# A two-layer hybrid decoder trunk on one core: weight places 448 columns wide, compressed products on four column groups, the last tile's scores cut in two, and a new order table

## The chip, the cores and the metric

The kernel runs on one core of a Trainium2 chip. A core has five engines that run side by side, each through its own instructions in order: TensorE (PE, matrix products and transposes), VectorE (DVE), ScalarE (ACT), GpSimd (POOL) and SyncE (SP, here the one that starts nearly all loads and stores). They wait for one another by semaphores. TensorE multiplies a stationary operand, which it loads first (PEld, at most 128 columns), with a moving operand of at most 512 columns, and writes to PSUM, a small memory of 8 banks of 512 float32 columns; all other data lie in SBUF.

The metric is device time in microseconds (us) of one execution, as the median of several.

## The reference

512 tokens of width 1024 pass two layers. A layer normalizes x, multiplies by one wide matrix w_in, and hands the columns to four groups of mixers:

```python
h = rmsnorm(x, norm_w)
p = split_cols(h @ w_in)
o_a = dsa_mixer(...)       # ReLU indexer, top 128 keys of each query, softmax attention
o_b = nsa_mixer(...)       # compressed, selected and window attention, gated
o_c = shortconv_mixer(...) # b * conv3(c * x)
o_d = pool_mixer(...)      # pooling over 2, 4, 8, 16 tokens, minus the token, a product, a scale
x + concat(silu(gate) * o) @ w_out
```

Group B's compressed branch makes 32 (31 used) compressed keys and values out of blocks of 32 tokens at a stride of 16, each by one product with a 2048 x 64 matrix, and attends to them:

```python
blocks = tok[:, cmp_idx] + pe_cmp
return blocks.reshape(B, n_cmp, CMP_LEN * HEAD_DIM) @ w     # compress
s_c = jnp.einsum('bqhd,bnd->bhqn', qb, k_cmp) * scale
```

All values are float32, and the output must keep nearly that precision.

## The kernel before, in words

**Tiling.** Tokens are cut into 4 tiles of 128; the 1024 channels into 8 chunks of 128 (`KC`). To keep precision on fast products, an operand is split into a high part (rounded for the fast product) and a low part (the difference), and a product becomes three: high x high, high x low, low x high. ACT writes the high part, POOL or VectorE the low part (`lo`). `lin_tok` (lines 639 to 648) gives token-major results, `lin_ch` (650 to 658) channel-major ones, 24 products of up to 512 columns each. Weights come through `load_w` (580 to 606): two chunks at a time land in a place `st` (3 of them), and go from there to `wh` and `wl` (6 of each). All these places are 436 columns wide, the widest that a load needs, and hold two rows of 436 float32: the second begins 1,744 bytes in.

**The order.** The kernel's functions don't issue anything. They record instructions on a `Tape`, numbered from 0 in the order in which Python meets them (5,023 of them). `ORDER` (lines 180 to 437) lists all numbers in the order in which `play` (515 to 536) then issues them, and so fixes each engine's order, and which buffer of its kind each tile gets (`place`). Engines take their own instructions in that order; a wait at the head of an engine's queue holds everything behind it.

**A layer.** `projections` (1336) runs the indexer's, group A's and group B's projections, transposes the queries and keys, and computes the index scores. Then, in program order, come `compress` and `compressed`, the gates of A and B, `channel_constants` (in layer 0), attention of A and B tile by tile, with the top-k searches (`topk`, 16 rounds of VectorE's MAX8 and MATCH_REPLACE8) between them, convolution, pooling, and the output projection. The order table interleaves all that, so that TensorE has long products while softmax pieces come back from the other engines.

**Compressed products.** `compress` (1018) makes the two token streams `u` (keys s=0, values s=1). `compressed` (1035 to 1066) loads the 2 x 2048 x 64 matrices into four places (`wt` for the first 8 steps, `st` for the last 8) and does 16 steps t, with two full-precision products each: 32 stationary columns of `u`, 64 moving columns of weights, one for the keys into PSUM partitions 0 to 31 and one for the values into 32 to 63. `tape.after` chains them so that the two alternate. Then ACT copies keys (`zc`) and values (`vc`), POOL rotates the keys (`rope`), TensorE transposes them, and ACT and VectorE write them as high and low part into `kcT`, which is columns 0 to 31 of the key tile `kTB`, ahead of the 512 token keys.

**Scores.** `probs` (1079 to 1116) does one branch of one tile: per head two products (high and low key part) into a PSUM bank `s` of 512 columns, then one VectorE reduction that adds the mask, writes `pb` and leaves the extreme in `mn`, and the exponential on ACT. For tiles 1 and 2 of group B the 32 compressed keys and the up to 384 token keys of the selected branch fit one bank, and both come from one product (`cmp`). For tile 3 they would be 32 + 512 = 544 columns; so `att_b` (1195) gives it a second bank `sc` of kind `tr`, with two products of 32 columns for each head, and one VectorE sum of 128 columns (`e`) for all heads.

**The start.** 40 transposes of the identity (`warm`, 685) are recorded at the start and stand where the order table puts them; `spread` (692) transposes norm weights (`g_row`, loaded by ACT's queue) and spreads them over partitions.

Of the kernel before, what the change touches and what calls it, by code (L numbers as in the profile page):

```python
# [13 lines left out]
OP = mybir.AluOpType  # L14
# [157 lines left out]
class Engine:  # L172
# [367 lines left out]
def trunk(ctx: ExitStack, tc: tile.TileContext, x, norm_w, w_in, w_out, conv_w, pe_cmp, w_cmp_k, w_cmp_v,  # L540
# [39 lines left out]
    def load_w(src, segs, early=None, start=False):  # L580


        n = sum(c for _, c in segs)
        stage = res.tile([P, KC, 436], F32, name=nm("ws"), tag=early) if early else None

        def part(h):
            if early:
# [278 lines left out]
    def layer(l, hT, w_first, norm):  # L866
# [168 lines left out]
        def compressed(us):  # L1035
# [13 lines left out]
            for t in range(16):  # L1049
                for s in range(2):  # L1050
                    op = PE.matmul(pc[32 * s : 32 * s + 32, 0:HD], us[s][:, t::16], wts[2 * (t // 8) + s][:, t % 8, :],
                                   start=t == 0, stop=t == 15)
                    if before:
                        tape.after(op, before)
# [434 lines left out]
```

## Time and profile before

| what | value |
|---|---|
| median of 3 runs | 520.76 us (519.15 to 520.86) |
| the profiled execution | 520.58 us, of it span 518.8 us |
| mean granted TensorE clock | 0.998 |
| loads and stores | 50.06 MB, mean 96 GB/s |
| compressed products' records | 128 (64 a layer) |
| records of 32-column scores | 16 (8 a layer) |

The span runs from the first instruction to the last; the rest of the execution's time lies around it. A row of the timeline gives start, duration, engine, operation, `out<-in` by the names of the program, rows*columns of the stationary operand, the moving operand and a count. A row of the groups gives busy time and mean duration in ns, and behind the bar the idle time ahead of the group with what ended it. TensorE's products overlap one another, so the distance between starts, not the duration, tells what one costs.

### The profile page before, as it was taken

What the parts mean: (1) busy time and instruction counts of PE and PEld (TensorE: products, weight loads), DVE (VectorE), ACT (ScalarE), POOL (GpSimd) and SP (SyncE); (2) the same over time, 40 slices, a digit from 0 to 9 for tenths busy, and PEclk for the clock granted to TensorE, in tenths of its full rate; (3) what the DMA queues carried; (4) which work ended last, traced back from release to release, by engine and by line L of the source; (5) the groups of instructions that cost most, each with busy time, mean ns of one, the idle gap of its engine ahead of it and who ended that gap; (6) DMA issues with size and microseconds to landing.
All of it is one profiled execution on the core that took longest, in us unless ns stands there. A gap on an engine that the chain in (4) does not pass through costs nothing. (4 is left out here: it accounts for less than half of the span.)

```text
span 518.8 us, 8976 instructions
## 1 busy us (share of the span) xinstructions
PE 509.1 (98%) x2691; PEld 425.4 (82%) x2691; DVE 374.2 (72%) x1038; ACT 337.7 (65%) x840; POOL 316.4 (61%) x541
## 2 busy tenths in 40 slices
PE   8999999999999999999999999999999999999995
PEld 7998787888888888887888988877888888888885
DVE  5536999998888684872571599999984786868523
ACT  5889866444568877675478993464566787787522
POOL 5799843664375938747388972256456578584531
PEclk9999999999999999999999999999999999999999
DMA  7954531553321102205865431055241302022304
GB/s 245 246 116 128 124 97 22 140 138 79 79 58 36 61 23 63 61 27 153 283 188 150 111 92 31 2 151 127 52 119 32 92 1 65 18 81 62 134 9 162
DMA packets 73247, 50.06 MB, mean 96 GB/s; under 512 B 24680, under 2 KB 63728, under 8 KB 73200
## 3 DMA queue, kind: packets, MB, share of 16 engines
q1 hardware_dynamic: 72608, 48.45, 34.8%
q10 hardware_dynamic: 592, 1.05, 0.5%
q8 instruction: 21, 0.34, 0.3%
q14 instruction: 26, 0.21, 0.1%
HBM read 45.29 MB, written 4.19 MB: 95 GB/s over the span
## 5 line engine op out<-in xcount | busy, mean ns | idle before, releaser
L535 PE MATMUL mm<-hT,wh 128*128 128x512 f32 x544 | 172.8, 401 | 0.3 <-DVE sg L535 0.3
L535 POOL TENSOR_TENSOR wl<-st,wh 128x384 fp32r<-128x384 f32 (+2 forms) x116 | 110.0, 969 | 61.2 <-ACT wh L535 56.8
L535 PEld LDWEIGHTS mm<-hT,wh 128*128 128x128 f32 x544 | 100.4, 188 | 20.9 <-DVE sg L535 1.1
L535 PE MATMUL mm<-w,mT 128*128 128x512 f32 (+1 forms) x408 | 100.5, 385 | 0.3 <-DVE cd L535 0.3
L535 PE MATMUL mm<-hT,wl 128*128 128x512 f32 x272 | 98.9, 400 | 0.3 <-DVE sg L535 0.3
L535 PEld LDWEIGHTS mm<-w,mT 128*128 128x128 f32 x408 | 72.2, 188 | 15.0 <-DVE cd L535 0.5
L535 POOL TENSOR_TENSOR w<-st,w 128x512 fp32r<-128x512 f32 x48 | 61.8, 1300 | 21.8 <-ACT w L535 19.8
L535 ACT ACTIVATE wh<-st 128x768 fp32r<-128x768 f32 (+2 forms) x60 | 47.3, 790 | 24.1 <-DMA st<-in_w_in_dram 14.5
L535 PEld LDWEIGHTS mm<-hT,wl 128*128 128x128 f32 x272 | 50.6, 188 | 10.6 <-issue 0.4
L535 ACT ACTIVATE pb<-pb,mn 128x512 f32<-128x512 f32 (+3 forms) x96 | 53.2, 556 | 8.7 <-DVE mn L535 8.3
L535 PE MATMUL mm<-wh,hT 128*128 128x436 f32 (+1 forms) x224 | 52.9, 336 | 0.8 <-DVE vA L535 0.4
L535 POOL TENSOR_SCALAR pb<-pb,rs,gt 128x512 f32<-128x512 f32 (+3 forms) x64 | 38.4, 616 | 23.3 <-DVE rs L535 14.8
L535 DVE MAX8 m<-acc 128x8 f32<-128x384 f32 (+2 forms) x96 | 51.5, 551 | 0.8
L535 DVE MATCH_REPLACE8 acc<-m,acc 128x384 f32<-128x384 f32 (+2 forms) x96 | 51.9, 543 | 0.3
L535 PE MATMUL mm<-w,hT 128*128 128x512 f32 x192 | 51.9, 399 | 0.0
L535 DVE TENSOR_TENSOR pl<-tr,ph 128x512 fp32r<-128x512 f32 x60 | 40.2, 682 | 7.0 <-ACT ph L535 5.7
L535 ACT ACTIVATE ph<-tr 128x512 fp32r<-128x512 f32 x60 | 34.5, 593 | 13.6 <-PE tr L535 13.4
L535 DVE CUSTOM_DVE_ANT_0 pb<-s,mask 128x512 f32<-128x512 f32 (+3 forms) x64 | 30.6, 486 | 16.8 <-PE s L535 11.0
L535 PEld LDWEIGHTS mm<-w,hT 128*128 128x128 f32 x192 | 34.7, 189 | 6.9 <-issue 0.3
L535 PEld LDWEIGHTS mm<-wh,hT 128*128 128x128 f32 x224 | 37.6, 188 | 3.1 <-DVE vA L535 0.7
L535 PE MATMUL tr<-ident,pb 128*128 128x128 f32 x240 | 39.6, 273 | 0.0
L535 ACT ACTIVATE w<-st 128x512 fp32r<-128x512 f32 x48 | 29.6, 626 | 9.8 <-DMA st<-in_w_out_dram 4.9
(174 smaller groups left out, 920.0 us busy)
## 6 DMA issues: line engine op xcount, KB each, us to landing
st<-in_w_in_dram SPq DMA_DIRECT2D x136, 128.0 KB, 2.6
st<-in_w_out_dram SPq DMA_DIRECT2D x32, 256.0 KB, 2.9
st<-in_w_in_dram SPq DMA_DIRECT2D x24, 256.0 KB, 2.9
x<-in_x_dram SPq DMA_DIRECT2D x16, 256.0 KB, 3.6
x1d<-x SPq DMA_DIRECT2D x8, 256.0 KB, 3.6
x<-x1d SPq DMA_DIRECT2D x8, 256.0 KB, 3.4
ws<-in_w_in_dram SPq DMA_DIRECT2D x4, 384.0 KB, 4.8
st<-in_w_in_dram SPq DMA_DIRECT2D x4, 384.0 KB, 3.4
```

The costliest lines, as they stand in the source:

```text
L535: getattr(self.engines[op.eng].real, op.name)(*[real(a) for a in op.args], **{k: real(v) for k, v in op.kw.items()})
```

## The change

- `load_w`: the places `ws`, `st`, `wh` and `wl` become 448 columns wide (1,792 bytes a row, 14 x 128). What is loaded and computed in them stays.
- `compressed`: steps are taken two at a time, t and t+1. Keys and values of the even steps go to PSUM partitions 0 to 31 and 32 to 63 as before, those of the odd steps to 64 to 95 and 96 to 127, so that four column groups take turns. ACT then copies the upper half (`odd`, 64 x 64), and VectorE adds it to the lower one.
- `probs` and `att_b`: where compressed and token keys don't fit one bank (tile 3), they are cut in two halves of 272 columns, each with two products, a bank and a reduction of its own; the second reduction starts from the first one's extreme. The separate bank `sc`, its products of 32 columns and the sum over all heads go; each head has a sum of 32 columns.
- `channel_constants`: the pool weights are no longer made ready for both layers in layer 0, but in each layer for itself (`pool_weights`), in tiles of half the size.
- `ORDER` is replaced by a table of 5,044 numbers; nearly every instruction stands a few places elsewhere on its engine.

```diff
 ORDER = [
...
 ]
...
-        stage = res.tile([P, KC, 436], F32, name=nm("ws"), tag=early) if early else None
+        stage = res.tile([P, KC, 448], F32, name=nm("ws"), tag=early) if early else None
...
-                st = wp.tile([P, 2, 436], F32, name=nm("st"), tag="st", bufs=3)
+                st = wp.tile([P, 2, 448], F32, name=nm("st"), tag="st", bufs=3)
...
-            wh = wp.tile([P, 2, 436], F32R, name=nm("wh"), tag="wh", bufs=6)
-            wl = wp.tile([P, 2, 436], F32R, name=nm("wl"), tag="wl", bufs=6)
+            wh = wp.tile([P, 2, 448], F32R, name=nm("wh"), tag="wh", bufs=6)
+            wl = wp.tile([P, 2, 448], F32R, name=nm("wl"), tag="wl", bufs=6)
...
+    def pool_weights(l):
+        st = wp.tile([P, 2, P], F32, name=nm("st"), tag="st", bufs=3)
+        G.memset(st, 0.0)
+        for j in range(2):
+            for h in range(2):
+                SP.dma_start(st[64 * h : 64 * h + 64, j, 64 * h : 64 * h + 64], pool_w[l, 2 * j + h])
+        pw[:] = [const.tile([P, 2, P], F32R, name=nm("pw"), tag=f"pw{s}") for s in range(2)]
         S.activation(pw[0], st, AF.Copy)
         lo(G, pw[1], st, pw[0])
...
-            for t in range(16):
-                for s in range(2):
-                    op = PE.matmul(pc[32 * s : 32 * s + 32, 0:HD], us[s][:, t::16], wts[2 * (t // 8) + s][:, t % 8, :],
-                                   start=t == 0, stop=t == 15)
-                    if before:
-                        tape.after(op, before)
-                    before = op
+            for t in range(0, 16, 2):
+                for e in range(2):
+                    for s in range(2):
+                        o = 2 * e + s
+                        op = PE.matmul(pc[32 * o : 32 * o + 32, 0:HD], us[s][:, t + e :: 16],
+                                       wts[2 * (t // 8) + s][:, (t + e) % 8, :], start=t == 0, stop=t == 14)
+                        if before:
+                            tape.after(op, before)
+                        before = op
+            odd = wk.tile([HD, HD], F32, name=nm("odd"), tag="om", bufs=1)
+            S.activation(odd, pc[HD:P, 0:HD], AF.Copy)
+            V.tensor_add(pc[0:HD, 0:HD], pc[0:HD, 0:HD], odd)
...
+            cuts = [(0, c + n)] if c + n <= T else [(0, (c + n) // 2), ((c + n) // 2, c + n)]
...
-                ps = bank("s", 2)
-                PE.matmul(ps[:, : c + n], qT[m, i][:, h, :], kT[0][:, : c + n], start=True, stop=False)
-                PE.matmul(ps[:, : c + n], qT[m, i][:, h, :], kT[1][:, : c + n], start=False, stop=True)
-                if sc is not None:
-                    o = sc[:, 32 * h : 32 * h + 32]
-                    PE.matmul(o, qT[m, i][:, h, :], kcT[0], start=True, stop=False)
-                    PE.matmul(o, qT[m, i][:, h, :], kcT[1], start=False, stop=True)
-                if cmp:
-                    cmp(h, ps[:, 0:32])
-                V.tensor_tensor_reduce(out=p, in0=ps[:, c : c + n], in1=bias, scale=-0.125 if gcol else 0.125, scalar=3.0e38,
-                                       op0=OP.add, op1=OP.min, accum_out=mn[:, h : h + 1])
+                low = 3.0e38
+                for a, b in cuts:
+                    ps = bank("s", 2)
+                    PE.matmul(ps[:, : b - a], qT[m, i][:, h, :], kT[0][:, a:b], start=True, stop=False)
+                    PE.matmul(ps[:, : b - a], qT[m, i][:, h, :], kT[1][:, a:b], start=False, stop=True)
+                    if cmp and a == 0:
+                        cmp(h, ps[:, 0:32])
+                    o = c if a == 0 else 0
+                    keys = slice(a + o - c, b - c)
+                    V.tensor_tensor_reduce(out=p[:, keys], in0=ps[:, o : b - a], in1=bias[:, keys],
+                                           scale=-0.125 if gcol else 0.125, scalar=low, op0=OP.add, op1=OP.min,
+                                           accum_out=mn[:, h : h + 1])
+                    low = mn[:, h : h + 1]
...
-            joint = 32 + n <= T
-            sc = None if joint else bank("tr", 3)
-            pb = probs("b", i, [k[:, 1, 0 if joint else 32 :] for k in kTB], mask[:, T - n :], 2,
-                       cmp if joint else None, sc)
-            if not joint:
-                V.tensor_add(e, sc[:, 0:P].rearrange("p (h n) -> p h n", h=NH),
-                             cbias[:, i, None, :].to_broadcast([P, NH, 32]))
+            pb = probs("b", i, [k[:, 1, :] for k in kTB], mask[:, T - n :], 2, cmp)
```

More of the change, by code (lines that the diff above doesn't have):

```diff
@@ L722, in trunk @@
     gcol = const.tile([P, DEPTH - 1, KC], F32, name="gcol")
-    pw = [const.tile([P, DEPTH, 2, P], F32R, name=f"pw{s}") for s in range(2)]
+    pw = []
     e_spread = [const.tile([P, NH, P], F32R, name="es")]
@@ L751, in channel_constants @@
     def channel_constants():
-        st = wp.tile([P, DEPTH, 2, P], F32, name=nm("st"), tag="st", bufs=3)
-        G.memset(st, 0.0)
         for l in range(DEPTH):
@@ L756, in channel_constants @@
                 SP.dma_start(cw[:, l, :, j], conv_w[l, :, j * P : (j + 1) * P].rearrange("t p -> p t"))
-                for h in range(2):
-                    SP.dma_start(st[64 * h : 64 * h + 64, l, j, 64 * h : 64 * h + 64], pool_w[l, 2 * j + h])
             SP.dma_start(psc[:, l, :], pool_scale[l].rearrange("(j p) -> p j", p=P))
@@ L1077, in gates, with probs @@
             V.scalar_tensor_tensor(sg[m][:, j, :], sg[m][:, j, :], 1.0, ps, op0=OP.add, op1=OP.mult)
-        def probs(m, i, kT, bias, gcol, cmp=None, sc=None):
+        def probs(m, i, kT, bias, gcol, cmp=None):
             n = P * (i + 1)
             c = 32 if cmp else 0
+            cuts = [(0, c + n)] if c + n <= T else [(0, (c + n) // 2), ((c + n) // 2, c + n)]
             per = T // n if n <= T // 2 else 1
@@ L1322, in conv_gate_pool @@
             pm = bank("tr", 3)
-            PE.matmul(pm, pw[0][:, l, j, :], ah, start=True, stop=False)
-            PE.matmul(pm, pw[0][:, l, j, :], al_, start=False, stop=False)
-            PE.matmul(pm, pw[1][:, l, j, :], ah, start=False, stop=True)
+            PE.matmul(pm, pw[0][:, j, :], ah, start=True, stop=False)
+            PE.matmul(pm, pw[0][:, j, :], al_, start=False, stop=False)
+            PE.matmul(pm, pw[1][:, j, :], ah, start=False, stop=True)
             V.scalar_tensor_tensor(pm, pm, psc[:, l, j : j + 1], b, op0=OP.mult, op1=OP.mult)
@@ L1359, in layer @@
             channel_constants()
+        pool_weights(l)
         w = load_w(win, [(B_GATE, 256)])
```

513 rows, old and new, of the table ORDER are left out of this document.

## The prediction, made before the changed kernel ran

> **What bounds the kernel now.** I read the head of the page first, then the waits of TensorE. Every row carries line 535, because one helper issues all instructions; the names of the tiles tell the work apart.
>
> ```profile
> span 518.8 us, 8976 instructions
> PE 509.1 (98%) x2691; PEld 425.4 (82%) x2691; DVE 374.2 (72%) x1038; ACT 337.7 (65%) x840; POOL 316.4 (61%) x541
> ```
>
> ```profile
> PE tr L535 <- POOL ident L535: 1.5, 1, 1.5
> PE mm L535 <- DVE sg L535: 0.7, 2, 0.3
> PE mm L535 <- DVE vA L535: 0.4, 1, 0.4
> ```
>
> TensorE is busy for 98% of the span. In the list of its waits (engine, who, whom, us in total) 1.5 us fall at the very start, and after that no entry is over 0.7; four that I leave out have 0.3 or less each. So at most 2.3 us of the rest is waiting, and the kernel lasts as long as TensorE's own instructions. What takes time off TensorE shortens the span; what is added to the other engines is free until one of them makes TensorE wait.
>
> **The compressed products.** Timeline around them in the second layer (start, duration, form, count), then durations (min/median/max) of three kinds of products:
>
> ```profile
> 338.82 0.39 PE L535 MATMUL mm<-hT,wh 128*128 128x512 f32 x1
> 339.05 0.62 PE L535 MATMUL mm<-hT,wl 128*128 128x512 f32 x2
> 339.60 1.21 PE L535 MATMUL tr<-wt,u 128*32 128x64 f32 x32
> 340.65 1.12 PE L535 MATMUL tr<-st,u 128*32 128x64 f32 x32
> 342.11 0.47 PE L535 MATMUL mm<-hT,wl 128*128 128x512 f32 x1 [0.34 <-DVE sg L535]
> ```
>
> ```profile
> L535 PE MATMUL mm<-wl,hT x2: 280/280/280, 14.2 to 14.4; 128*128 128x256 f32 x2
> L535 PE MATMUL mm<-wl,hT x2: 355/358/360, 27.8 to 28.6; 128*128 128x436 f32 x2
> L535 PE MATMUL tr<-st,u x8: 220/221/223, 340.7 to 340.9; 128*32 128x64 f32 x8
> ```
>
> Durations overlap, so I count starts. The first half begins at 339.60 and the second at 340.65: 32 records in 1.05 us, 33 ns each, 2.1 us for the 64 records of a layer. There are 32 products, hence two records each. Does one record fill those 33 ns alone? The 436-wide product lasts 78 ns longer than the 256-wide: 0.43 ns a column. The full-precision record of 64 columns lasts 59 ns less than the 256-wide, as if it had 256 - 59/0.43 = 119 columns, and 119 columns are 52 ns of array time. A record of 52 ns that comes every 33 ns means that 1.6 run at once: the two column groups of today overlap. With four groups in turn I take four records in the time that two need now: 64 records in about 1.05 us, 1.02 us saved a layer, **2.05 us** in all. The bounds are no gain at all (a third and a fourth group don't overlap) and this 1.02 a layer; I take the upper end, because the rows show overlap already. The stop before and after the stage (0.34 us here) stays.
>
> The two half sums must now be added: an ACT copy and a VectorE sum of 64x64 stand between the products and the keys.
>
> ```profile
> 93.00 0.21 ACT L535 ACTIVATE vc<-tr 32x64 fp32r<-32x64 f32 x1 [0.99 <-PE tr L535]
> 94.32 0.24 POOL L535 TENSOR_TENSOR zc<-r,r 32x32 f32<-32x32 f32 x1
> 97.44 0.25 PE L535 MATMUL tr<-ident,zc 32*128 32x32 f32 x1
> ```
>
> In the first layer the rotated keys are ready at 94.56 and transposed at 97.44: 2.9 us of slack. The two additions cost about 0.21 each, plus what stands ahead on VectorE; the queued product work covers them. Counting in the order tables, 18 products stand between the stage and that transpose afterwards, 19 before. In the second layer more than 100 do. Next in line are the last tile's scores: their first halves now hold the compressed keys, so they wait for this chain; the new table puts them 15 products (3.5 us) behind the transpose. I cost this at nothing; without cover it is a few tenths a layer.
>
> **The last tile's scores.** Today each of 4 heads in 2 layers does two products of 512 and two of 32 columns; then it does four of 272. Timelines of the first layer's 32-wide products and of 288-wide ones:
>
> ```profile
> 115.80 0.62 PE L535 MATMUL mm<-hT,wh 128*128 128x512 f32 x2
> 116.26 0.27 PE L535 MATMUL tr<-ident,pb 128*128 128x128 f32 x1
> 116.29 0.37 PE L535 MATMUL tr<-kTB,qb 128*128 128x32 f32 x2
> 116.51 0.47 PE L535 MATMUL mm<-hT,wh 128*128 128x512 f32 x1
> 116.82 0.18 PE L535 MATMUL tr<-kTB,qb 128*128 128x32 f32 x1
> 116.85 0.31 PE L535 MATMUL tr<-ident,pb 128*128 128x128 f32 x1
> 116.92 0.26 PE L535 MATMUL tr<-kTB,qb 128*128 128x32 f32 x1
> 117.03 0.95 PE L535 MATMUL mm<-hT,wh 128*128 128x512 f32 x3
> ```
>
> ```profile
> 409.03 0.56 PE L535 MATMUL s<-kTB,qb 128*128 128x288 f32 x3
> 409.43 0.63 PE L535 MATMUL mm<-hT,wl 128*128 128x512 f32 x2
> ```
>
> A 512-wide product takes 0.23 (338.82 to 339.05). From 115.80 to 117.03 three of them and six short ones take 1.23, so the six take 0.54; the 117.03 group also holds its first product about 0.08 longer. That makes 0.09 to 0.10 for each short one, whatever its width. Three of 288 take 0.40, 0.133 each; at (0.23 - 0.133)/224 a column, 272 take 0.126. A head falls from 2 x 0.23 + 2 x 0.10 = 0.66 to 4 x 0.126 = 0.50; eight times 0.16 is **1.3 us** (1.1 to 1.4).
>
> **VectorE pays.** Groups by form, the tile view of e, the read of an accumulator, and VectorE's share in two stretches (PE, PEld, DVE, ACT, POOL):
>
> ```profile
> L535 DVE CUSTOM_DVE_ANT_0 pb<-s,mask 128x512 f32<-128x512 f32 x16 | 10.9, 688 | 6.4 <-PE s L535 4.5 <-PE tr L535 1.8
> L535 DVE CUSTOM_DVE_ANT_0 pb<-s,mask 128x256 f32<-128x256 f32 x16 | 6.7, 420 | 0.9 <-PE s L535 0.5 <-PE tr L535 0.3
> L535 DVE TENSOR_TENSOR e<-s,cbias x24: 159/184/192, 153.4 to 452.5; 128x32 f32<-128x32 f32 x24
> L535 DVE TENSOR_TENSOR e<-tr,cbias x2: 274/283/292, 126.0 to 381.5; 128x128 f32<-128x128 f32 x2
> 94.47 0.08 DVE L535 DVE_READ_ACCUMULATOR2_ANT mn<- 128x1 f32 x1
> 52.00:78.00 26.00, 26.00 (x122) 21.03 (x121) 24.85 (x79) 18.99 (x55) 16.80 (x31) 1.00 0.44 109
> 312.00:339.00 27.00, 27.00 (x120) 22.04 (x119) 26.22 (x80) 11.45 (x27) 7.02 (x13) 1.00 0.07 15
> ```
>
> Eight reductions of 688 become sixteen of about 420: +1.2 us, and 8 x 0.08 for the accumulators, +0.6. One sum of 283 a layer becomes four of 184: +0.9. With the two new sums of about 0.2 that is 3.1 us, 1.6 a layer. VectorE is 96% and 97% busy in these stretches, but TensorE doesn't wait for it there, since top-k searches fill its queue ahead of their need. I cost it at nothing; without that cover it is the slower rival below.
>
> **The rest.** Moving the pool weights into each layer halves the first layer's memset, copy and difference and adds the same halves, with four small loads on SP's queue, to the second; POOL (61%) and ACT (65%) have the room. For places of 448 columns I expect nothing:
>
> ```profile
> L535 POOL TENSOR_TENSOR wl<-st,wh x20: 1007/1022/1037, 100.4 to 149.0; 128x384 fp32r<-128x384 f32 x20
> ```
>
> Every second of these 20 works on the row that begins 1,744 bytes in, off any multiple of 128, and all lie within 3%; the 436-wide products above also alternate between the two rows, within 5 ns.
>
> **The order table** moves nearly every instruction a few places. In the middle it can win at most the 2.3 us of waits and can add as much; I take 0. At the start it does something definite:
>
> ```profile
> 1.48 2.18 PE L535 MATMUL tr<-ident 128*128 128x128 f32 x9 [1.48 <-POOL ident L535]
> 3.59 0.27 PE L535 MATMUL tr<-ident,g_row 8*128 8x8 f32 x1
> 5.13 0.40 PE L535 MATMUL tr<-ident 128*128 128x128 f32 x2
> 7.86 0.93 PE L535 MATMUL tr<-ident 128*128 128x128 f32 x7
> 9.02 0.36 PE L535 MATMUL mm<-wl,hT 128*128 128x256 f32 x1 [0.23 <-POOL ss L535]
> ```
>
> Nine identity transposes now run from 1.48 at (2.18 - 0.42)/8 = 0.22 each; from about 5.13, 3.65 us after the first, they take (0.93 - 0.27)/6 = 0.11. The new table begins with the transpose of g_row, which waits for a load, so TensorE starts between 1.48 and 3.59; and 50 instructions stand ahead of the first real product, 43 today. If the slow rate again lasts 3.65 us, 17 run slow and 33 fast: first product 3.65 + 3.6 us after the start, at 8.7 to 10.8 instead of 9.02. Against that, in the new table less is left over behind it and the weights' differences come earlier. I take 0, with -1.0 and +1.8 as ends. The Trainium skill (TensorE: Matmul & The Clock Gate, Part 1) says that the clock is released after a busy window of about 3.4 us whose phase is free-running; the 3.65 us here agree, and by it a later start could also cost a second window.
>
> **Sum.** The profiled execution took 520.6 us (span 518.8 and 1.8 around it), 0.2 under the median of 520.76. 520.6 - 2.05 - 1.3 = **517.2 us**.
>
> **Rivals.**
> 1. *A floor on starts.* Four groups overlap, but records can't be issued at 16 ns. The closest starts above are 0.03 apart (116.26 and 116.29); the gain lies between 0 and 1.02 a layer, in the middle 0.5: 518.2. The Trainium skill (same page, "Wait — 56ns, not 53.3ns?") puts such a floor at about 25 ns, however narrow the product; by it 64 records take 1.6 us and the sum would be an estimated 518.3.
> 2. *Only two groups overlap.* The scores alone gain: 520.6 - 1.3 = 519.3. For it: no row shows more than two at once.
> 3. *Start or order lose.* The late clock costs 1.8: 519.0; or new waits of 2.2 us in the middle: 519.4.
> 4. *VectorE becomes the bound (slower).* In 52 to 78 us it has 1.15 us idle, in 312 to 339 0.8. If its results, not TensorE's queue, set the pace there, TensorE's gains are lost and the 3.1 us come on top: 523.7. It decides once a layer's 1.6 us more exceed that idle time and the search results are needed at once; against it, no wait of TensorE on a search result stands among the first rows.
>
> **How the numbers follow.** Forecast 0.48; rivals 0.17, 0.13, 0.16 (both parts together) and 0.06. The range 515.2 to 519.9 holds the forecast with the table's spread (2 us down), rivals 1 to 3, and leaves out rival 4 and some tails. About 0.5% (2.6 us) is what a measurement of this kernel can tell from no change, so faster begins at 518.2: four fifths of the forecast, half of rival 1, little of 2 and 3, 0.52; slower is rival 4, 0.06; 0.42 lies between.
>
> **What would show it.** Compressed stage: 64 records in 1.05 us (right), 1.6 to 2.1 (rivals 1, 2). Scores: no 32-wide products, four of 272 at 0.126. Start: the time of the first real product, and where the 0.22 become 0.11. TensorE's waits: a new entry on mn, e or m8 means rival 4; one on kTB means that the longer chain is late.

## The result, and the profile after

The changed kernel takes 513.66 us in the median of 4 runs (513.06 to 514.09), the kernel before 520.45 in the runs beside it; the ratio is 0.9873, with an interval of 0.9851 to 0.9895. A second set of runs gave 513.04 (0.9866, 0.9846 to 0.9886). The gain is 6.8 to 7.3 us, twice the 3.4 that the prediction summed up, and the time lies below its range. The profiled execution took 514.09 us.

The head of the page, and TensorE's waits (one of 0.2 left out):

```profile
span 512.4 us, 9015 instructions
...
PE 502.3 (98%) x2691; PEld 423.3 (83%) x2691; DVE 375.8 (73%) x1062; ACT 336.3 (66%) x843; POOL 315.1 (62%) x543
```

```profile
PE tr L536 <- DMA g_row<-in_norm_w_dram: 2.3, 1, 2.3
PE tr L536 <- DVE hT L536: 0.6, 1, 0.6
PE mm L536 <- ACT wh L536: 0.3, 1, 0.3
PE mm L536 <- DVE sg L536: 0.2, 1, 0.2
```

TensorE is still the bound (98%), with the same 2,691 records, in 6.8 us less busy time. No entry on mn, e, m8 or kTB has appeared: VectorE did not become the bound (busy 1.6 us more, where 3.1 were forecast), and the longer chain to the compressed keys is not late.

The compressed products of the second layer (timeline: start, duration, form, count):

```profile
336.18 0.78 PE L536 MATMUL tr<-wt,u 128*32 128x64 f32 x32
336.76 0.72 PE L536 MATMUL tr<-st,u 128*32 128x64 f32 x32
337.42 1.66 PE L536 MATMUL mm<-hT,wh 128*128 128x512 f32 x6
```

The second half starts 0.58 us after the first, where it was 1.05: 18 ns a record instead of 33. Four groups do overlap, much as forecast. The last tile's scores in the first layer:

```profile
124.23 0.39 PE L536 MATMUL mm<-hT,wl 128*128 128x512 f32 x1
124.46 0.41 PE L536 MATMUL s<-kTB,qb 128*128 128x272 f32 x2
124.70 0.39 PE L536 MATMUL mm<-hT,wl 128*128 128x512 f32 x1
```

Two products of 272 take 0.24 by the rounded rows (0.124 each in the trace), as forecast (0.126). So both named terms came. What the prediction lacks is elsewhere.

**Where else.** I looked at the longest unbroken series of equal products, the output projection near the end: 512-wide products of w and mT. First the kernel before, with a second series of it, then the changed kernel:

```profile
63.68 4.49 PE L535 MATMUL mm<-w,hT 128*128 128x512 f32 x19
...
483.13 17.10 PE L535 MATMUL mm<-w,mT 128*128 128x512 f32 x73
```

```profile
476.62 17.07 PE L536 MATMUL mm<-w,mT 128*128 128x512 f32 x74
```

The last product of a series lasts 0.39 to 0.40 by the model, so the starts lie (17.10 - 0.40)/72 = 231.9 ns apart before and (17.07 - 0.39)/73 = 228.5 after. And the kernel before has a series that runs at (4.49 - 0.40)/18 = 227.2. The three differ in where their operands lie. In the program's allocation the activations hT and mT of both kernels start 96 bytes past a multiple of 128. So do the weights of the series at 63.68, whose places are 16 KB long. The weights of the series at 483.13 lie 0, 32, 64 and 96 bytes past one, because their places are 3,488 = 27.25 x 128 bytes long. With 448 columns a place is 3,584 = 28 x 128 bytes, and all of them lie at 96. Three and a half ns on each of some 1,570 wide products would be 5 us. That became theory P (places); its rival was theory O: the new order takes small waits away.

### The profile page after: what moved, and what is told of

It reads as the page before. It is cut to its first block, busy times and chain, and to the rows that moved or that the text cites. A ratio compares the mean times of both kernels' runs of the same rounds, so it can differ in the third digit from the quotient of the medians.

```text
span 512.4 us, 9015 instructions
## 1 busy us (share of the span) xinstructions
PE 502.3 (98%) x2691; PEld 423.3 (83%) x2691; DVE 375.8 (73%) x1062; ACT 336.3 (66%) x843; POOL 315.1 (62%) x543
## 3 DMA queue, kind: packets, MB, share of 16 engines
q10 hardware_dynamic: 592, 1.05, 0.5%
## 4 chain that ended last, share of the span: by engine, by line
PE 91%; ACT 3%; DMA 2%; issue 1%; DVE 1%; POOL 1%; SPq 0%; POOLq 0%; ACTq 0%; DVEq 0%
PE mm L536 69%; PE tr L536 9%; PE s L536 7%; PE pv L536 6%; DMA st<-in_w_in_dram 2%; ACT wh L536 1%; POOL wl L536 0%; SPq L536 0%; ACT pb L536 0%; DVE xn L536 0%; ACT ph L536 0%; ACT xn L536 0%; POOL w L536 0%; POOL ss L536 0%; ACT tr L536 0%
## 5 line engine op out<-in xcount | busy, mean ns | idle before, releaser
L536 POOL TENSOR_TENSOR wl<-st,wh 128x384 fp32r<-128x384 f32 (+2 forms) x116 | 108.9, 960 | 62.9 <-ACT wh L536 60.5
L536 PE MATMUL mm<-w,mT 128*128 128x512 f32 (+1 forms) x408 | 102.5, 385 | 0.0
L536 DVE MAX8 m<-acc 128x8 f32<-128x512 f32 (+2 forms) x96 | 51.9, 552 | 0.9
L536 DVE MATCH_REPLACE8 acc<-m,acc 128x256 f32<-128x256 f32 (+2 forms) x96 | 51.9, 543 | 0.2
L536 PE MATMUL tr<-ident,pb 128*128 128x128 f32 x240 | 43.0, 272 | 0.0
L536 DVE CUSTOM_DVE_ANT_0 pb<-s,mask 128x256 f32<-128x256 f32 (+4 forms) x64 | 28.2, 449 | 12.4 <-PE s L536 6.5
L536 PEld LDWEIGHTS tr<-ident,pb 128*128 128x128 f32 x240 | 30.8, 140 | 7.9 <-POOL pb L536 0.6
```

Of the source, the lines that this page charges most:

```text
L536: getattr(self.engines[op.eng].real, op.name)(*[real(a) for a in op.args], **{k: real(v) for k, v in op.kw.items()})
```

## Experiments

Every run has its own runs of the kernel before beside it (519.0 to 522.3, medians 520.3 to 520.8). Times are medians in us, with the ratio's interval in brackets.

**Only the width undone.**

```diff
-            wh = wp.tile([P, 2, 448], F32R, name=nm("wh"), tag="wh", bufs=6)
+            wh = wp.tile([P, 2, 436], F32R, name=nm("wh"), tag="wh", bufs=6)
...
```

(wl, st and the early stage likewise.) 

> The changed kernel with its order table, four groups and score cut, but the staging and weight places 436 columns wide again (3,488 bytes, so that the places start at 0, 32, 64 and 96 bytes past a multiple of 128, and the second row of a place at 80 bytes past its first). Theory P (places): the unforeseen 3.4 us come from the places; between two 512-wide products the start-to-start time was 232 ns in the median before and is 228 now, and about 1,400 wide products at 2.5 ns each make 3.5 us. Then this kernel takes 517.2 (516.5 to 518) and the median spacing is 232 again. Theory O (order): the new table took away small waits; then the width does nothing, 513.7 (513.0 to 514.4), and the spacing stays at 228.

515.42, ratio 0.9905 (0.9890 to 0.9921): 1.8 to 2.4 more than the changed kernel, which theory O does not allow, though less than P's 3.5; the time lies between the two expected ranges. The slower series is back:

```profile
477.53 17.05 PE L536 MATMUL mm<-w,mT 128*128 128x512 f32 x73
```

(17.05 - 0.40)/72 = 231.3 ns between starts.

**All places moved to a multiple of 128 bytes.**

```diff
-far = const.tile([P, 1], F32, name="far")
+far = const.tile([P, 9], F32, name="far")[:, 0:1]
```

> The changed kernel with one constant tile 32 bytes longer, so that all wide places start at a multiple of 128 bytes; in the changed kernel all of them start 96 bytes past one. If what counts is that all places lie alike, 513.7 (513.2 to 514.2) with the same spacing of 227 to 228. If the distance to the 128-byte boundary itself counts, another spacing: at a multiple the products read one line less, up to 2 ns each, 511 to 513; or the 96 was the lucky one, 515 to 517.

512.92, ratio 0.9858 (0.9840 to 0.9875): as the changed kernel (513.66 and, in its second set, 513.04). The number also lies within the 511 to 513 that were expected for an effect of the boundary, so the spacing decides: in the stretch shown for the next two runs the starts are 227.5 ns apart here and 226.7 in the changed kernel. The runs show no effect of the 128-byte boundary itself, nor of a line less to read.

**Weights and work places moved by 32 bytes against the activations.**

```diff
-vc = res.tile([P, P], F32R, name=nm("vc"), tag="vc")
+vc = res.tile([P, P + 8], F32R, name=nm("vc"), tag="vc")[:, 0:P]
```

> The changed kernel with one tile in front of the weight places 32 bytes longer: all weight and work places start at a multiple of 128 bytes, while the activations hT, mT, kTA, kTB and vB stay 96 bytes past one. All places of one kind still lie alike, but the two operands of most products lie apart. If what matters is that an operand's rows sit regularly by themselves: 513.7 (513 to 514.3), spacing 227 to 228. If the two operands of a product must lie alike: 516 to 517.5, spacing 232.

516.75, ratio 0.9931 (0.9917 to 0.9944). **By 64 bytes** (P + 16):

> The changed kernel with all weight and work places moved by 64 bytes against the activations (they were moved by 32 in the run that took 516.75). If the operands' difference counts modulo 64 bytes: 513.3 (512.8 to 514.0), spacing 227 to 228. If it counts modulo 128, and every difference but zero costs the same: 516.0 to 517.2, spacing 232. In the records of the kernel before, products whose operands lie 64 bytes apart stand at 231.3 in the mean, against 232.8 at 32 and 230.7 at zero: by that, between, 514.5 to 516.

517.15, ratio 0.9929 (0.9914 to 0.9944). The longer `vc` moves what lies behind it: all of wh and wl, and with them all 816 wide products of hT with wh and wl. Of the 360 wide products of w and mT it moves the weights of 276, and of the 192 of w and hT none. A stretch of hT with wh and wl in the first layer, its first and its last row: in the changed kernel, moved by 32 and moved by 64.

```profile
102.94 0.39 PE L536 MATMUL mm<-hT,wl 128*128 128x512 f32 x1
...
113.82 0.39 PE L536 MATMUL mm<-hT,wl 128*128 128x512 f32 x1
```

```profile
102.89 0.40 PE L536 MATMUL mm<-hT,wl 128*128 128x512 f32 x1
...
114.09 0.40 PE L536 MATMUL mm<-hT,wl 128*128 128x512 f32 x1
```

```profile
102.55 0.39 PE L536 MATMUL mm<-hT,wl 128*128 128x512 f32 x1
...
113.75 0.39 PE L536 MATMUL mm<-hT,wl 128*128 128x512 f32 x1
```

From the first to the last start there are 48 products of 512 columns, without a wait: 10.88/48 = 226.7 ns, and 11.20/48 = 233.3 in both moved kernels. The groups by form say the same, with products that were not moved beside those that were (changed kernel, then moved by 32):

```profile
L536 PE MATMUL mm<-hT,wh 128*128 128x512 f32 x544 | 172.1, 399 | 0.2 <-DVE sg L536 0.2
L536 PE MATMUL mm<-w,hT 128*128 128x512 f32 x192 | 52.2, 398 | 0.0
```

```profile
L536 PE MATMUL mm<-hT,wh 128*128 128x512 f32 x544 | 173.8, 402 | 0.2 <-DVE sg L536 0.2
L536 PE MATMUL mm<-w,hT 128*128 128x512 f32 x192 | 52.4, 398 | 0.0
```

The places are as long and as regular as in the changed kernel, only their distance to the activations is no longer zero modulo 128, and 3.1 to 4.1 us are lost, more than by the narrow places, of which a part still lies alike. The rule modulo 64 falls.

**The places alone, in the old order.** The old program has no room for 448 columns unless the pool weights are loaded by layer, so this was done too; every instruction that both have keeps its place in the old order.

```diff
-pw = [const.tile([P, DEPTH, 2, P], F32R, name=f"pw{s}") for s in range(2)]
+pw = []
...
-            wh = wp.tile([P, 2, 436], F32R, name=nm("wh"), tag="wh", bufs=6)
+            wh = wp.tile([P, 2, 448], F32R, name=nm("wh"), tag="wh", bufs=6)
...
+        pool_weights(l)
```

> The kernel before, in its own order, with its two column groups and its scores in 512 and 32; only the places are 448 wide, and the pool weights go into each layer to make the room. The runs so far say that it is not the 128-byte boundary that counts but that the weights and activations of a product lie alike, and put the places at 2.1 us. Then 518.1 (517.5 to 518.7), with 227 to 229 ns between 512-wide products. If the places pay only together with the new order: 520.3 (519.8 to 520.9).

523.78, slower (1.0062, 1.0049 to 1.0075), but by a wait of my own making:

```profile
PE s L531 <- DVE acc L531: 5.0, 1, 5.0
```

```profile
ACT pw L531 <- DMA st<-in_pool_w_dram: 5.1, 1, 5.1
```

ScalarE stood 5.1 us at the second layer's pool weights, whose copy follows right behind their four loads in this order, and what was queued behind it held VectorE and then TensorE. With some 100 places between them:

> The kernel before, in its own order, with places of 448 and the pool weights of each layer loaded by themselves; the second layer's copy now stands some 100 instructions behind its loads, so that ScalarE doesn't wait for them. If the places act by themselves: 518.0 (517.0 to 518.7), 227 to 229 ns between 512-wide products. If they pay only together with the new order: 520.3 (519.8 to 521).

516.52, ratio 0.9917 (0.9903 to 0.9931), below the range expected: with the places alone the kernel is **3.8 to 4.2 us** under the medians of the kernel before, more than half of the gain. The moved pool weights are in that number; a run with them and narrow places wasn't made. The kernel before and this one run the same products in the same order, so their groups by form compare line by line (busy us, then the modelled mean of one); the kernel before first:

```profile
L535 PE MATMUL mm<-hT,wh 128*128 128x512 f32 x544 | 172.8, 401 | 0.3 <-DVE sg L535 0.3
L535 PE MATMUL mm<-hT,wl 128*128 128x512 f32 x272 | 98.9, 400 | 0.3 <-DVE sg L535 0.3
L535 PE MATMUL mm<-w,mT 128*128 128x512 f32 x360 | 95.1, 399 | 0.3 <-DVE cd L535 0.3
L535 PE MATMUL mm<-w,hT 128*128 128x512 f32 x192 | 51.9, 399 | 0.0
```

```profile
L531 PE MATMUL mm<-hT,wh 128*128 128x512 f32 x544 | 171.6, 399 | 0.5 <-DVE sg L531 0.5
L531 PE MATMUL mm<-hT,wl 128*128 128x512 f32 x272 | 98.2, 397 | 0.5 <-DVE sg L531 0.5
L531 PE MATMUL mm<-w,mT 128*128 128x512 f32 x360 | 94.1, 396 | 0.0
L531 PE MATMUL mm<-w,hT 128*128 128x512 f32 x192 | 51.4, 397 | 0.0
```

418.7 against 415.3, 3.4 us, in means that differ by 2 or 3 ns of 400. Of these, 0.5 us stand in the products of w and hT, whose operands lie alike in both kernels; their own operands' position doesn't explain that part. The series at the end shows it plainer, (17.20 - 0.39)/74 = 227.2 ns:

```profile
479.15 17.20 PE L531 MATMUL mm<-w,mT 128*128 128x512 f32 x75
```

**The order alone**, carried over to the old program, once with its narrow places and once with 448 columns:

```diff
 ORDER = [
-    3, 4, 2, 0, 609, 5, 1, 55, 6, 57, 82, 56, 7, 890, 894, 8, 608, 9, 93, 596,
+    3, 4, 2, 0, 603, 607, 55, 1, 604, 597, 58, 608, 93, 592, 593, 82, 600, 601, 605, 120,
...
```

> The kernel before (places of 436, two groups, scores in 512 and 32) with the new order carried over to its instructions; the 32-wide score products stand together behind the last head. By difference: the changed kernel's 513.3, plus 2.1 for the places, 1.7 for the groups and 1.3 for the scores, so 518.4 (517.7 to 519.2), which gives the new order some 1.9 us. If the parts are not additive and the order alone is nothing: 520.3 (519.8 to 521).

> The same program (two groups, scores of 512 and 32, places of 448) with the new order carried over. If places and order add up: 520.2 less 2.1 to 2.7, so 517.7 (517.0 to 518.3), equal to the run beside it within 0.7. If the order pays only where the products run evenly, it is 1 to 2 us below the run beside it, 516.0 to 516.9.

520.16 beside 520.44 (0.9988, 0.9977 to 1.0000), and 515.66 beside the 516.52 above: the order, its start included, is worth 0.3 to 0.9 us, the first hardly told from nothing, and less than the 1.9 that the differences had given. In the first of the two TensorE waits 0.9 for a probability tile (pb), which it doesn't in the second; with it gone the order might be worth that much more, which wasn't tried.

**The other way round**, the old order carried over to the changed program, whole and in three stretches without the last tile's scores:

> The changed kernel with places of 448, four groups and score cut, but with the order of the kernel before, carried over to its instructions: every instruction that both kernels have keeps its place in the old sequence, but for some ten products around the last tile's scores, which had to make room; the new instructions stand right behind what they need. Theory P: spacing of 512-wide products stays at 227 to 228 ns, and the time is that of the changed kernel with what the order is worth, at most 1.5 us more: 513.2 to 515.2. Theory O: 516.5 to 518, with the new waits spread over the middle, and the spacing at 232.

> The changed kernel, with the order of the kernel before in the three stretches that hold no scores of the last tile (orders 400 to 1050, 1500 to 3430 and 4150 to the end, about three quarters of the program); start and the two score stretches keep the new order. Theory O: the new table saves the small waits there, 1.5 to 2.5 us, so 515.2 to 516.2, and TensorE's loss against its own product times rises in these stretches. Theory P (the places did nearly all that the prediction lacked): 513.5 to 514.2.

537.76 and 532.88, and neither says anything of the order: the first rows of their waits, in this sequence, are

```profile
PE tr L532 <- POOL pb L532: 7.8, 2, 5.9
PE s L532 <- DVE mn L532: 3.2, 6, 1.0
```

```profile
PE pv L532 <- ACT ph L532: 4.3, 1, 4.3
```

which neither kernel has. My guess is that they come where old and new pieces meet, since scores cut in two need two banks and two reductions a head where the old order left room for one; that isn't shown. What they do show: in the first of them the 512-wide series again runs even in the old order, at (22.40 - 0.39)/97 = 226.9 ns.

```profile
499.92 22.40 PE L532 MATMUL mm<-w,mT 128*128 128x512 f32 x98
```

**The start.** The old order in the first 400 instructions, and then only nine identity transposes moved ahead of the one that waits (the diff is that of the second, against the changed kernel):

```diff
 ORDER = [
...
-    94, 45, 105, 56, 5, 57, 46, 598, 6, 121, 106, 7, 48, 59, 8, 107, 9, 54, 117, 10,
+    94, 5, 6, 7, 8, 9, 10, 11, 12, 13, 45, 105, 56, 57, 46, 598, 121, 106, 48, 59,
...
```

> The changed kernel with the order of the kernel before in its first 400 instructions (about the first 18 us): TensorE begins with the transposes of the identity, which need no load. If the new start cost what its profile shows (first product at 2.30 instead of 1.48, first real product at 11.35 instead of 9.02; 5.96 us lost in the first 20 us, 4.80 before), 512.3 to 512.8. If that time is made good by the work that is queued behind, or if the instant at which the clock is released decides and wanders from run to run, 513.2 to 514.2.

> The changed kernel with nine transposes of the identity moved ahead of the transpose that waits for a load, and nothing else: TensorE starts at about 1.5 instead of 2.3 to 3.2 us, and the faster rate begins that much earlier. If the start of TensorE is on the path: 0.8 to 1.5 us less, 511.8 to 512.5. If the run with the old start shows the rule (2.0 us less lost in the first 20 us, then 1.8 us of waiting for vA at 43.9 us), the early start is given back there: 513.0 to 513.6.

The first took 515.02 (0.9902, 0.9887 to 0.9917), 1.4 to 2.0 more than the changed kernel and above both expected ranges: TensorE reached its first real product at 8.52 and later stood:

```profile
43.94 0.70 PE L532 MATMUL mm<-w,hT 128*128 128x512 f32 x2 [1.75 <-DVE vA L532]
```

The second took 513.34 (0.9861, 0.9847 to 0.9874) with the first transpose at 1.47 and the first real product at 9.98: no gain in the median. The base for these, the changed kernel once more:

> The changed kernel itself, once more, as the base for the three runs beside it: 513.7 (513.0 to 514.2). Whatever differs from the earlier runs of it is the error of a comparison across chips.

513.04 (512.15 to 514.67).

**The groups alone.**

```diff
-                        o = 2 * e + s
+                        o = s
...
-            V.tensor_add(pc[0:HD, 0:HD], pc[0:HD, 0:HD], odd)
+            V.tensor_tensor(pc[0:HD, 0:HD], pc[0:HD, 0:HD], odd, OP.max)
```

> The changed kernel, but the compressed products go to the two column groups of before, all 16 steps accumulating there; the copy and the second VectorE operation stay in the chain as a maximum with itself, so that the number of instructions is the same. As in the prediction: 64 records take 2.1 us a layer instead of 1.05 to 1.2, so 515.6 (515.2 to 516.0). Rival: the products' time is hidden or the chain of additions decides, then 513.7.

515.04, ratio 0.9891 (0.9875 to 0.9907), 1.4 to 2.0 above the changed kernel; its first layer:

```profile
92.17 1.17 PE L536 MATMUL tr<-wt,u 128*32 128x64 f32 x32
93.17 1.40 PE L536 MATMUL tr<-st,u 128*32 128x64 f32 x32
```

The halves lie 1.00 apart again.

**The scores cut at 512 and 32.**

```diff
-            cuts = [(0, c + n)] if c + n <= T else [(0, (c + n) // 2), ((c + n) // 2, c + n)]
+            cuts = [(0, c + n)] if c + n <= T else [(0, T), (T, c + n)]
```

> The changed kernel, but the last tile's scores are cut at 512 and 32 columns instead of twice 272; the number and order of all instructions is unchanged. By the prediction's own sum a head then takes 0.66 again instead of 0.50, eight heads 1.3 us: 514.6 (514.3 to 515.0). If the cut was hidden behind VectorE: 513.3.

515.70, ratio 0.9908 (0.9894 to 0.9921): 2.0 to 2.7 above the changed kernel, not 1.3. Two places of its timeline:

```profile
123.49 0.39 PE L536 MATMUL mm<-hT,wl 128*128 128x512 f32 x1
123.72 0.29 PE L536 MATMUL s<-kTB,qb 128*128 128x32 f32 x2
123.86 0.48 PE L536 MATMUL mm<-hT,wl 128*128 128x512 f32 x1
124.17 0.40 PE L536 MATMUL mm<-hT,wh 128*128 128x512 f32 x1
...
126.03 0.63 PE L536 MATMUL mm<-hT,wl 128*128 128x512 f32 x2
126.67 0.37 PE L536 MATMUL s<-kTB,qb 128*128 128x32 f32 x2
```

From 123.49 to 124.17 two wide products (0.454 at 0.227) and two short ones take 0.68: 0.113 for a short one. Most of that is not in its own record: its successor comes 0.03 or 0.11 later, and the wide product after it, 0.48 instead of 0.39 long, is held by 0.09. With 0.113 a head gains 2 x 0.227 + 2 x 0.113 - 4 x 0.124 = 0.18, and eight heads 1.5 us. The rest is this kernel's own: at 126.03 two products take 0.64 instead of 0.45, 0.19 more, and so at three heads. The profile names nothing that they wait for; that the bank for the second cut isn't free yet is a guess.

## Why the prediction was wrong

- **What bounds the kernel:** right. TensorE is 98% busy before and after. But the sentence drawn from it, that "the kernel lasts as long as TensorE's own instructions", was only used for which instructions there are, not for how fast each of them runs.
- **Compressed products, 2.05:** right in mechanism and nearly in size. The halves lie 0.58 apart instead of 1.05 (0.53 was forecast), and undoing the groups costs 1.4 to 2.0. The floor on starts (rival 1) and the two groups (rival 2) fall: 18 ns a record is also below the 25 that rival 1 ends with.
- **Scores, 1.3:** right in mechanism, a little small. The mis-sized term is a short product's "0.09 to 0.10": it is 0.113, so 1.5.
- **VectorE at nothing, the longer chain at nothing, the pool weights at nothing:** no wait of TensorE on any of them in the profile after.
- **The step that failed:** "For places of 448 columns I expect nothing." It stood on a POOL operation and on the modelled durations of the 436-wide products, "within 5 ns". That yardstick was too coarse: 2.5 ns on 1,570 products is 3.9 us, more than the whole forecast. It also looked at the wrong thing, the row within a place, when the starts of TensorE's own products depended on how weights and activations lie to each other. The runs showed 3.8 to 4.2 us in its place in the old order, 1.8 to 2.4 when the width was undone in the changed kernel, and 3.1 to 4.1 when weights and activations were moved apart. The clue was in the trace of before: 227.2 ns at 63.68, 231.9 at 483.13.
- **The order:** middle taken at 0 with 2.3 either way; the whole table measured 0.3 to 0.9 of gain. The start was taken at 0, with a first real product at 8.7 to 10.8. It came at 11.35 in the profiled execution and at 11.50 in the second set's, with a slow rate that lasted 5.8 us there and not 3.65 (below). What the new start alone is worth, no run shows: with the old one the kernel lost 1.4 to 2.0, but there TensorE waited 1.8 for vA.

Along one path the parts add up: 520.4, less 3.9 for the places, less 0.9 for the order, less 2.0 to 2.6 for groups and scores together (515.66 to the changed kernel's 513.0 to 513.7). Undone one by one in the changed kernel, places, groups and scores cost 1.8 to 2.4, 1.4 to 2.0 and (less the 0.56 of its own waits) 1.5 to 2.1. So groups and scores gave about 1 us less together than the 3.35 forecast for them, and the places less in the changed kernel than in the old one. I haven't settled these remainders; single runs of one kernel spread over 0.5 to 2.5 us.

## What to carry to other kernels

Where one engine is full, ask not only which instructions it runs but whether equal ones run equally fast: compare the start-to-start time of long unbroken series of the same product, and if they differ by one or two per cent, look at the addresses. Then try lengths that are multiples of 128 bytes for buffers whose tiles meet in one product, so that all of them keep the same position modulo 128; here the position itself (0 or 96) made no difference. A tolerance has to be multiplied by the count before it is called nothing.

## What was not expected of the hardware

**Operands that lie alike.** A stretch of 512-wide products ran at 226.7 ns where all operands lay at the same position modulo 128 bytes, and at 233.3 where weights and activations lay 32 or 64 bytes apart, which cost 3.1 to 4.1 us in the changed kernel. In the old order, with the same products, places of 448 are worth 3.8 to 4.2 us of 520. But a product's own two operands are not all of it. I gave each record its operands' addresses in the program and counted distances of up to 240 ns: in the kernel before, a product follows its predecessor after 230.9 ns in the mean where the operand that is loaded next lies like the one that streams, and after 232.8 where it lies 32 bytes further. In the two moved kernels the products of w and mT that still lie alike follow one another after 230.8, and those moved by 64 bytes also after 230.8. So alike operands among others that aren't alike don't reach 227, and which neighbours count is open. The Trainium skill (SBUF — State Buffer, "Operand start alignment") asks only that an operand start at a multiple of its element size and says of its runs that they timed nothing, so it speaks neither for nor against; what in the chip makes the difference, no run here shows.

**The clock's release wanders.** The same order, in the changed kernel and with the narrow places:

```profile
2.30 0.24 PE L536 MATMUL tr<-ident,g_row 8*128 8x8 f32 x1 [2.30 <-DMA g_row<-in_norm_w_dram]
...
6.58 1.49 PE L536 MATMUL tr<-ident 128*128 128x128 f32 x6
...
8.46 1.36 PE L536 MATMUL tr<-ident 128*128 128x128 f32 x11
...
11.05 0.44 PE L536 MATMUL tr<-ident,xn 128*128 128x128 f32 x2 [0.57 <-DVE hT L536]
...
11.35 0.36 PE L536 MATMUL mm<-wh,hT 128*128 128x256 f32 x1
```

```profile
2.31 0.24 PE L536 MATMUL tr<-ident,g_row 8*128 8x8 f32 x1 [2.31 <-DMA g_row<-in_norm_w_dram]
...
6.16 0.82 PE L536 MATMUL tr<-ident 128*128 128x128 f32 x6
...
9.88 0.37 PE L536 MATMUL mm<-wh,hT 128*128 128x256 f32 x1
```

At 6.58 the transposes still take (1.49 - 0.42)/5 = 0.21 in the one; at 6.16 they take (0.82 - 0.27)/5 = 0.11 in the other. The faster rate begins about 3.4 us after the first transpose with the narrow places and 5.8 in the changed kernel, and the first real product comes 1.5 us earlier or later, of which 0.6 is the wait for hT. The prediction had worked with 3.65 alone. The Trainium skill (TensorE: Matmul & The Clock Gate, Part 1) calls the window free-running, and these executions agree. It also fits that an earlier first transpose bought nothing in the median; that this is the reason isn't shown.
